# Strassen's scheme for four more blocks of the down projection in the first feed-forward group

## The chip, the cores and the metric

The kernel runs on one core of one Trainium2 chip, in one launch. The time is the device time of that launch in microseconds (us). Beside it stands a profile of one execution on the same chip. The engines: PE multiplies matrices and loads its weights by instructions of their own (PEld), DVE and ACT do elementwise work, POOL some small copies, and SP issues most of the DMA transfers. Every engine takes its own instructions in order and waits at semaphores for the others.

## The reference

One step of a hybrid encoder layer over 2048 prompt tokens and 64 sample tokens, with a model width of 1024. The change touches only the second half, the gated feed-forward with a causal convolution of width 3 (`d_ff` = 2816):

```python
h2 = rmsnorm(x, g2) * (1 + sc2) + sh2
up = h2 @ w_up                                  # 1024 -> 2 * 2816
conv = b_conv + sum(w_conv[j] * upp[:, j:j + T] for j in range(3))
a, g = jnp.split(conv, 2, -1)
x = x + gt2 * ((jax.nn.silu(g) * a) @ w_down)   # 2816 -> 1024
```

All of it is float32. The kernel splits each operand into a high and a low part and takes three matmuls for each product of two blocks (high by high, high by low, low by high).

## The kernel before

The first third of the span is the attention and pooling half. Then the 2112 tokens run through the feed-forward in three groups (`fgroups`, `o.g` = 0, 1, 2) of 704 tokens. Channels lie on the partitions, tokens on the free axis. The 2816 hidden channels are 22 blocks of 128 (`f` = 0 to 21), and each block has an up-projection pair, one half for `a` and one for `g`.

**Up.** `Pair.products` (L1701) computes one pair by seven products in place of eight (Strassen's scheme in Winograd's form; the weight sums are ready in HBM as `wsum`, the sums of the activations in `B`). A product is 12 matmuls of 128x352, at L1604, and takes one "unit" of weights: 512 columns, loaded by SP, copied to the high part by ACT (L427), and turned into the low part by DVE (L430, "split" below). In group 0 all seven units of a pair are split, and three of them stored for the later groups (`wsplit`); groups 1 and 2 load those three as they are and split four. The results are taken from PSUM by DVE (`sum_g1` and `sum_a`, L1613, writing `eg` and `ea`) and ACT, run through the convolution (DVE L1582, four of them for a pair), Silu (ACT L1801), the gate (DVE L1806 or L1809), and a split into high and low (ACT L1884 and DVE L1889) into a tile called `av`. The steps of a pair lie in the products of the next one and the one after.

**The order of a pair's evacuation.** At the start of a pair its first product B11 is issued on PE; then come `sum_g1` and `sum_a` of the pair before. PE needs the first of them two products later, since the last product (T4) of the pair before goes into the same PSUM bank, and the second for a free bank.

**Down.** `PARTS` (L33) cuts the 22 blocks into parts. For group 0 they are (0, 5), (5, 10), (10, 16), (16, 22). After the pairs of a part its blocks are multiplied by `w_down`. A plain part is `down` (L2199): for each of 8 output blocks, each hidden block, two token ranges (448 and 256) and three passes, one matmul at L2212. A part of exactly four blocks (`NQ`) in groups 1 and 2 is a quad: its four blocks and the 8 output blocks are two Strassen products (`quad_down`, L2046), 14 half products of 6 matmuls of 128x352 for each, at L2073. It is held until after the first pair of the next part, whose evacuation is woven into it. A quad needs more of DVE and ACT: sums of the blocks and their splits (`step_2` to `step_7`, L1817, L1821, L1833) before it, and 24 additions to the residual in place of 16 behind it (`rows_add`, L2042).

**The sums of the quads' weights.** The four sums of each quad's weights are computed in the kernel by `quad_sums` (L1654): 10 pieces `d` (two for a quad), each in two column halves, 20 units in all. A unit is a load of 512 KB from `w_quad` into a tile of the `av` pool, four DVE operations of 128x256 on it (tile name `qs`, L1664 to L1670), and a store of 512 KB to `dsum`. It is a generator in the background list `bg[0]`: each `tick(0)` runs it to the next `yield`. A product ticks it twice (`if kc % 2: tick(0)`), a plain `down` once in every 12 matmuls. In `bg[1]` runs `prepare`, which makes the next group's activations and their sums (DVE L747, L784, L780 on `fscr`). `drain(i)` runs a list to its end.

**What sets the order.** PE, ACT, DVE and POOL keep the order of the program (`manual_schedule`, L2032); only SP's order is chosen by a scheduler. Weights are loaded up to seven units ahead and split up to three ahead (`ahead[:] = [7, 4, WB, 1]`); `wt` tiles number 7, `raw` tiles 5, `av` tiles 7, PSUM banks for this work 6.

Of the kernel before, what the change touches and what calls it, by code (L numbers as in the profile page):

```python
# [31 lines left out]
ENDS = ((0, 448), (448, 704))  # L32
PARTS = (((0, 5), (5, 10), (10, 16), (16, 22)), ((0, 4), (4, 8), (8, 12), (12, 16), (16, 20), (20, 22)),  # L33
         ((0, 4), (4, 8), (8, 12), (12, 16), (16, 22)))
NQ, QUADS = 4, 5


def paired(g, part):
    return g > 0 and part[1] - part[0] == NQ
EPS = 1e-6  # L40
# [25 lines left out]
def tile_layer(ctx: ExitStack, tc: tile.TileContext, xT, vecs, cst, rst, w_mod, w_ada, w_qkou, w_v, w_pool,  # L66
# [38 lines left out]
    bg = ([], [], [], [], [])  # L105
# [1547 lines left out]

    def quad_sums():  # L1654

        for d in range(2 * QUADS):
            for c in (0, 256):
                t = f2.tile([P, 2, FT], F32R, tag="av", name="qs", bufs=AVB)
                w = t.bitcast(F32).rearrange("p a t -> p (a t)")[:, :1024].rearrange("p (i c) -> p i c", i=4)
                nc.sync.dma_start(out=w, in_=w_quad[d, :, :, c:c + 256])  # L1660
                for _ in range(5):
                    yield
# [10 lines left out]
                nc.sync.dma_start(out=dsum[d, :, :, c:c + 256], in_=w)  # L1673
                yield
                yield
# [476 lines left out]
    for o in fgroups:  # L2152
        Bo = B[o.g]
        held = None
        for pi, part in enumerate(PARTS[o.g]):
# [4 lines left out]
            av = [None] * nf  # L2160
            quad = Quad() if paired(o.g, part) else None
            if pi == 0:
                pair = None
            for f in range(f0, f1_):
                old, pair = pair, Pair(o, Bo, f, f - f0, av, quad)
                pair.products(old)
                if o.g == 0 and len(x3) < KD or pi == 0 and not bg[0]:
                    x3 += load_x2(o, range(len(x3), min(len(x3) + 2, KD)))
                if held is not None and nf > 2:
                    quad_down(o, held, pair, old)  # L2170
                    held = None
            if pi == 0 and o.g > 0:
                drain(0)
                x3 += load_x2(o, range(len(x3), KD))
            if not o.last:
                if pi == 0:
                    if o.g == 0:
                        bg[0].append(quad_sums())
                    bg[1].append(prepare(fgroups[o.g + 1], fscr))
                if lastp:  # L2180
                    drain(0, 1)
                    if nf == 2:
# [94 lines left out]
        if not o.last:  # L2277
            drain(1)
            if nf == 2:
                Bn = B[-1]  # L2280
                Bn.load(BN[-1])
            bg[0].append(final(o, x3, ssum, nf == 2))
            x3 = []
# [87 lines left out]
```

## Time and profile before

| what | value |
| --- | --- |
| median of 3 runs | 2170.43 us (2169.34 to 2173.03) |
| the profiled execution's own time | 2169.81 us |
| its span, first to last instruction | 2168.0 us |
| group 0's pairs and down parts | from 789 to 1252 us of the span |
| PE busy in 745 to 1257 us | 510.66 of 512.00 us |
| DVE busy in 745 to 1257 us | 396.88 of 512.00 us |
| ACT busy in 745 to 1257 us | 281.42 of 512.00 us |
| share of the DMA engines' time in 745 to 1257 us | 0.83, at 285 GB/s |
| granted PE clock there | 1.00 |

A row of the windows view names a stretch of the span, its length, then each engine's busy time with the number of its instructions, the granted PE clock, the share of the DMA engines' time and the rate. A row of the timeline has a start, a duration, the engine, the line, the operation, the tiles and shapes, and in brackets the idle time just before it with what ended it. Two operations of one engine can overlap in their records: the distance from one start to the next is what the engine needed. A row of the chain of waits has a start, a length, and the engine and line that set the end there.

### The profile page before, as it was taken

What the parts mean: (1) busy time and instruction counts of PE and PEld (TensorE: products, weight loads), DVE (VectorE), ACT (ScalarE), POOL (GpSimd) and SP (SyncE); (2) the same over time, 40 slices, a digit from 0 to 9 for tenths busy, and PEclk for the clock granted to TensorE, in tenths of its full rate; (3) what the DMA queues carried; (4) which work ended last, traced back from release to release, by engine and by line L of the source; (5) the groups of instructions that cost most, each with busy time, mean ns of one, the idle gap of its engine ahead of it and who ended that gap; (6) DMA issues with size and microseconds to landing.
All of it is one profiled execution on the core that took longest, in us unless ns stands there. A gap on an engine that the chain in (4) does not pass through costs nothing.

```text
span 2168.0 us, 38128 instructions
## 1 busy us (share of the span) xinstructions
PE 2146.5 (99%) x13529; PEld 2040.9 (94%) x13529; DVE 1666.4 (77%) x3107; ACT 1104.1 (51%) x2201; POOL 249.3 (12%) x468
## 2 busy tenths in 40 slices
PE   8999999999999999999999999999999999999998
PEld 7888888888899999999999999999999999999998
DVE  5777678677675878797968668988888797887874
ACT  4554335334333556464736445655656455565554
POOL 0010000001000301010101220100101121111112
PEclk9999999999999999999999999999999999999999
DMA  8987997897788686888968976666666875555542
GB/s 317 330 307 228 321 317 252 282 320 269 246 286 281 229 268 232 293 288 301 353 235 307 319 264 206 226 227 200 219 232 230 277 269 190 171 175 188 173 157 76
DMA packets 302439, 545.28 MB, mean 252 GB/s; under 512 B 25984, under 2 KB 118656, under 8 KB 302248
## 3 DMA queue, kind: packets, MB, share of 16 engines
q1 hardware_dynamic: 291656, 517.64, 70.6%
q10 hardware_dynamic: 10592, 25.20, 3.0%
q8 instruction: 107, 1.75, 0.3%
q14 instruction: 84, 0.69, 0.1%
HBM read 414.65 MB, written 128.08 MB: 250 GB/s over the span
## 4 chain that ended last, share of the span: by engine, by line
PE 60%; DVE 3%; DMA 1%; issue 1%; ACT 1%; POOL 0%; SPq 0%; DVEq 0%; POOLq 0%; ACTq 0%
PE mm L1604 37%; PE mm L2212 11%; PE mm L2073 10%; PE mm L494 2%; DVE wt L430 1%; DVE tg L1582 0%; ACT tg L1577 0%; DMA wt<-dsum 0%; DMA wt<-wsum 0%; DMA fscr<-h2d 0%; DVE ea L1613 0%; DVE eg L1613 0%; DVE x L2042 0%; DVE tg L1809 0%; ACT mm L1652 0%
## 5 line engine op out<-in xcount | busy, mean ns | idle before, releaser
L1604 PE MATMUL mm<-hx,wt 128*128 128x352 f32 x5544 | 887.1, 321 | 0.9 <-DVE wt L430 0.7
L1604 PEld LDWEIGHTS mm<-hx,wt 128*128 128x128 f32 x5544 | 880.5, 188 | 2.2 <-DVE wt L430 1.9
L494 PE MATMUL mm<-hl,wt 128*128 128x512 f32 (+2 forms) x1920 | 385.8, 356 | 0.3 <-DMA wt<-hl_kept 0.3
L427 ACT ACTIVATE wt<-raw 128x512 fp32r<-128x512 f32 (+3 forms) x468 | 275.9, 597 | 191.0 <-PE mm L494 53.4
L430 DVE TENSOR_TENSOR wt<-raw,wt 128x512 fp32r<-128x512 f32 (+3 forms) x468 | 307.3, 663 | 74.8 <-ACT wt L427 73.3
L494 PEld LDWEIGHTS mm<-hl,wt 128*128 128x128 f32 x1920 | 314.7, 188 | 48.1 <-issue 4.4
L2073 PE MATMUL mm<-av,wt 128*128 128x352 f32 x1512 | 248.2, 324 | 2.7 <-DVE ea L1613 1.2
L2073 PEld LDWEIGHTS mm<-av,wt 128*128 128x128 f32 x1512 | 242.3, 188 | 6.2 <-DVE ea L1613 4.0
L2042 DVE SCALAR_TENSOR_TENSOR x<-mm,MOD,x 128x352 f32<-128x352 f32 (+5 forms) x384 | 180.3, 508 | 69.0 <-PE mm L2212 54.1
L2212 PE MATMUL mm<-av,wt 128*128 128x448 f32 (+1 forms) x1440 | 232.2, 322 | 0.0
L2212 PEld LDWEIGHTS mm<-av,wt 128*128 128x128 f32 x1440 | 221.2, 188 | 9.9
L1652 ACT ACTIVATE mm<-mm 128x352 f32<-128x352 f32 x204 | 91.4, 448 | 235.9 <-PE mm L1604 176.6
L494 PE MATMUL mm<-mx,wt 128*128 128x512 f32 (+1 forms) x960 | 182.2, 351 | 1.2 <-DVE scr L266 1.2
L494 PEld LDWEIGHTS mm<-mx,wt 128*128 128x128 f32 x960 | 158.5, 188 | 24.1 <-DVE scr L266 1.1
L1582 DVE SCALAR_TENSOR_TENSOR ta<-ea,V,ta 128x704 f32<-128x704 f32 (+1 forms) x132 | 125.6, 952 | 54.8 <-ACT ta L1577 48.2
L1582 DVE SCALAR_TENSOR_TENSOR tg<-eg,V,tg 128x704 f32<-128x704 f32 (+1 forms) x132 | 125.7, 952 | 50.5 <-ACT tg L1577 48.0
L430 DVE TENSOR_TENSOR wt<-wt 128x512 fp32r<-128x512 f32 x204 | 138.4, 683 | 11.6 <-ACT wt L427 11.6
L427 ACT ACTIVATE wt<-wt 128x512 fp32r<-128x512 f32 x204 | 123.6, 622 | 34.0 <-DMA wt<-wsum 31.0
L1560 POOL COPY ea<-UC 128x2 f32<-128x2 f32 x66 | 32.7, 496 | 510.4 <-DVE ta L1582 429.1
L1801 ACT ACTIVATE tg<-tg 128x704 f32<-128x704 f32 (+1 forms) x66 | 52.4, 794 | 69.3 <-DVE tg L1582 69.3
L1143 PE MATMUL mm<-wt,hl 128*128 128x256 f32 (+1 forms) x576 | 71.2, 284 | 0.0
L1143 PEld LDWEIGHTS mm<-wt,hl 128*128 128x128 f32 x576 | 70.2, 189 | 0.8 <-issue 0.6
(306 smaller groups left out, 2220.2 us busy)
## 6 DMA issues: line engine op xcount, KB each, us to landing
wt<-wsplit SPq DMA_DIRECT2D x132, 512.0 KB, 4.3
raw<-w_up SPq DMA_DIRECT2D x198, 256.0 KB, 4.3
wt<-hl_kept SPq DMA_DIRECT2D x96, 512.0 KB, 6.3
wt<-wsum SPq DMA_DIRECT2D x132, 256.0 KB, 5.2
wsplit<-wt SPq DMA_DIRECT2D x66, 512.0 KB, 5.4
w<-w_up SPq DMA_DIRECT2D x88, 256.0 KB, 4.8
wsum<-w SPq DMA_DIRECT2D x44, 512.0 KB, 6.0
Bd<-fscr ACTq DMA_DIRECT2D x56, 352.0 KB, 4.4
```

The source lines that it names most:

```text
L427: act.activation(u.w[:, 0, :u.n], u.raw[:, :u.n], AF.Copy)
L430: dve.tensor_tensor(out=u.w[:, 1, :u.n], in0=u.raw[:, :u.n], in1=u.w[:, 0, :u.n].bitcast(F32), op=ALU.subtract)
L494: pe.matmul(ps[bi][:, :hi - lo], U[:, a, k % 4 * P:(k % 4 + 1) * P], mv[k][:, b, lo:hi], start=(at == 0 and pi == 0), stop=(k == order[-1] ...
L1143: pe.matmul(ps[ti][:n, :cols], h[4 * kh + k4][:, b, lo:lo + n], U[:, a, k4 % 2 * cols:(k4 % 2 + 1) * cols], start=(kh == 0 and k4 == 0 and ...
L1560: pool.tensor_copy(ext[:, 0:2], UC[:, f, :])
L1582: dve.scalar_tensor_tensor(out=t[:, :E], in0=ext[:, j:j + E], scalar=wc(j, f), in1=t[:, :E], op0=ALU.mult, op1=ALU.add)
L1604: pe.matmul(bk.t[:, :FH], U[:, a, kc * P:(kc + 1) * P], Bo.at(nm, kc, b), start=(first and kc == 0 and pi == 0), stop=(kc == 3 and pi == 2 ...
L1652: act.activation(to.t[:, :FH], bk.t[:, :FH], AF.Copy)
L1801: act.activation(self.tg[:, :E], self.tg[:, :E], AF.Silu)
L2042: dve.scalar_tensor_tensor(out=x3[n][:, a:b], in0=bk.t[:, a - lo:b - lo], scalar=gt2(n, s), in1=x3[n][:, a:b], op0=ALU.mult, op1=ALU.add)
L2073: pe.matmul(bk.t[:, :FH], U[:, a, c:c + P], quad.put(op, m, b), start=(first and m == 0 and pi == 0), stop=(m == 1 and pi == 2), skip_grou ...
L2212: pe.matmul(bks[i].t[:, :hi - lo], U[:, a, k % 4 * P:(k % 4 + 1) * P], av[k][:, b, lo:hi], start=(k == 0 and (a, b) == PASSES[0]), stop=(k ...
```

## The change

Group 0's parts become (0, 6), (6, 12), (12, 16), (16, 22), and the quad scheme is allowed for group 0 too, so that blocks 12 to 15 are a quad. Its weight sums (`d` = 6 and 7) must exist before, so the list of `quad_sums` is cut in two: `SUMS[0]` = pieces 6, 7, 0, 1, 2, 3 from the end of part 0's pairs on, and `SUMS[1]` = pieces 4, 5, 8, 9 after the quad has been multiplied. A `drain(0)` stands ahead of the quad's first pair, another after group 0's end. A unit of the list has 11 steps where it had 13 (4 empty ones for 5 after the load, 2 for 3 after the store).

```diff
-PARTS = (((0, 5), (5, 10), (10, 16), (16, 22)), ((0, 4), (4, 8), (8, 12), (12, 16), (16, 20), (20, 22)),
+PARTS = (((0, 6), (6, 12), (12, 16), (16, 22)), ((0, 4), (4, 8), (8, 12), (12, 16), (16, 20), (20, 22)),
          ((0, 4), (4, 8), (8, 12), (12, 16), (16, 22)))
 NQ, QUADS = 4, 5
+SUMS = ((6, 7, 0, 1, 2, 3), (4, 5, 8, 9))
 def paired(g, part):
-    return g > 0 and part[1] - part[0] == NQ
+    return part[1] - part[0] == NQ
...
-    def quad_sums():
-
-        for d in range(2 * QUADS):
+    def quad_sums(ds):
+
+        for d in ds:
             for c in (0, 256):
...
                 nc.sync.dma_start(out=w, in_=w_quad[d, :, :, c:c + 256])
-                for _ in range(5):
+                for _ in range(4):
                     yield
...
                 nc.sync.dma_start(out=dsum[d, :, :, c:c + 256], in_=w)
-                yield
                 yield
                 yield
...
             quad = Quad() if paired(o.g, part) else None
+            if quad is not None and o.g == 0:
+                drain(0)
...
                     quad_down(o, held, pair, old)
                     held = None
+                    if o.g == 0:
+                        bg[0].append(quad_sums(SUMS[1]))
...
                     if o.g == 0:
-                        bg[0].append(quad_sums())
+                        bg[0].append(quad_sums(SUMS[0]))
                     bg[1].append(prepare(fgroups[o.g + 1], fscr))
                 if lastp:
-                    drain(0, 1)
+                    drain(1) if o.g == 0 else drain(0, 1)
...
             drain(1)
+            if o.g == 0:
+                drain(0)
```

The program has 12 970 matmuls where it had 12 994: 168 more of 128x352 at the quad's line, 96 fewer of 128x448 and 96 fewer of 128x256. DVE has 3129 instructions for 3109, ACT 2217 for 2205 (eight PSUM copies more among them), SP 1540 for 1542. Lines behind the first edit are numbered one higher than before.

The first place is DVE in part 1, from one pair's evacuation (`eg`, `ea`) on. Before, in pair 6's work:

```order
L1613 TENSOR_TENSOR eg<-mm,s_10058 128x352
L1613 TENSOR_TENSOR ea<-mm,s_10058 128x352
L1806 TENSOR_TENSOR tg<-ta,tg 128x704
L430 TENSOR_TENSOR wt<-wt 128x512
L1889 TENSOR_TENSOR av<-tg,av 128x704
L430 TENSOR_TENSOR wt<-raw,wt 128x512
L1664 TENSOR_TENSOR qs<-qs 128x256
L1582 SCALAR_TENSOR_TENSOR ta<-ea,V,ta 128x704 x2
L430 TENSOR_TENSOR wt<-wt 128x512
L1666 TENSOR_TENSOR qs<-qs 128x256
```

The change, in pair 7's work (the second of its part, as pair 6 was before):

```order
L1614 TENSOR_TENSOR eg<-mm,s_10259 128x352
L1614 TENSOR_TENSOR ea<-mm,s_10259 128x352
L1806 TENSOR_TENSOR tg<-ta,tg 128x704
L431 TENSOR_TENSOR wt<-wt 128x512
L1665 TENSOR_TENSOR qs<-qs 128x256
L1667 TENSOR_TENSOR qs<-qs 128x256
L1889 TENSOR_TENSOR av<-tg,av 128x704
L431 TENSOR_TENSOR wt<-raw,wt 128x512
L1669 TENSOR_TENSOR qs<-qs 128x256
L1671 TENSOR_TENSOR qs<-qs 128x256
L1583 SCALAR_TENSOR_TENSOR ta<-ea,V,ta 128x704 x2
```

From this `eg` to the next one DVE has 24 instructions (7 of them `qs`), where it had 21 (4 `qs`); the next three distances have 23, 24 and 22 where the longest ones of the old part 1 had 21 and 23, and those of the old part 2 (pairs 10 to 15) 21, 21, 23 and 22.

The second place is DVE at the start of the new quad: what stands between `eg` of pair 15 and `eg` of pair 16, which is now inside `quad_down`. Of its 25 instructions these are the last:

```order
L1583 SCALAR_TENSOR_TENSOR tg<-eg,V,tg 128x704 x2
L785 TENSOR_TENSOR fscr<-fscr 128x352
L781 TENSOR_TENSOR fscr<-fscr 128x352
L431 TENSOR_TENSOR wt<-raw,wt 128x512
L431 TENSOR_TENSOR wt<-wt 128x512
L785 TENSOR_TENSOR fscr<-fscr 128x352
L781 TENSOR_TENSOR fscr<-fscr 128x352 x2
L1809 TENSOR_TENSOR tg<-ta,tg 128x704
L1821 TENSOR_TENSOR tg<-tg 128x352 x2
L431 TENSOR_TENSOR wt<-raw,wt 128x512
L1614 TENSOR_TENSOR eg<-mm,s_12117 128x352
L1614 TENSOR_TENSOR ea<-mm,s_12117 128x352
```

Before, pairs 15 and 16 lay on the two sides of a plain down part, and the end of pair 15's distance was:

```order
L784 TENSOR_TENSOR fscr<-fscr 128x352
L430 TENSOR_TENSOR wt<-raw,wt 128x512 x2
L1664 TENSOR_TENSOR qs<-qs 128x256
L1666 TENSOR_TENSOR qs<-qs 128x256
L784 TENSOR_TENSOR fscr<-fscr 128x352
L780 TENSOR_TENSOR fscr<-fscr 128x352
L430 TENSOR_TENSOR wt<-raw,wt 128x512
L430 TENSOR_TENSOR wt<-raw,wt 128x256
L1613 TENSOR_TENSOR eg<-mm,s_11866 128x352
```

What moved: no `qs` stands between pairs 12 and 16 any more, and in their place stand the gate, the differences of blocks (L1821) and their splits.

## The prediction

> **What bounds the kernel now.** I read the page's totals first, then the chain of waits through group 0, then the windows there pair by pair, and last the timeline of DVE.
>
> ```profile
> PE 2146.5 (99%) x13529; PEld 2040.9 (94%) x13529; DVE 1666.4 (77%) x3107; ACT 1104.1 (51%) x2201; POOL 249.3 (12%) x468
> ```
>
> PE is busy all the time but 21.5 us of the 2168.0, so time can only be won by taking matmuls away, and every new wait of PE costs its full length. What a matmul costs in a row of many is in the chain, whose pieces have a start, a length, a line and a count:
>
> ```profile
> 894.79 36.11 PE mm L1604 x228
> ...
> 1000.34 77.92 PE mm L1604 x492
> ...
> 1084.15 41.98 PE mm L2212 x264
> ...
> 1325.18 23.05 PE mm L2073 x144
> ```
>
> So an up matmul takes 77.92 / 492 = 0.158 us, a plain down matmul (448 and 256 columns by turns) 41.98 / 264 = 0.1590, one of a quad 23.05 / 144 = 0.1601. A pair of 7 x 12 matmuls is 84 x 0.158 = 13.3 us of PE.
>
> The whole-span 77% of DVE hides that DVE is full where the change puts work. The windows of one pair's length, first in the old part 1, then in the old part 2 (stretch, length, busy PE, PEld, DVE, ACT, POOL, clock, DMA share, GB/s):
>
> ```profile
> 934.00:947.00 13.00, 13.00 (x84) 12.98 (x83) 12.57 (x21) 10.02 (x19) 2.41 (x4) 1.00 0.95 323
> 947.00:960.00 13.00, 12.88 (x81) 12.57 (x80) 12.86 (x23) 9.75 (x18) 2.13 (x4) 1.00 0.96 349
> ...
> 1065.00:1078.00 13.00, 13.00 (x84) 13.00 (x83) 12.53 (x22) 9.37 (x18) 2.13 (x4) 1.00 1.01 351
> ```
>
> DVE works 12.5 to 12.9 of 13 us late in a part; PE loses its first 0.12 us at 947 to 960. I measure how late DVE is by the start of `eg`, which can start when the next pair begins on PE:
>
> ```profile
> 906.29 0.53 DVE L1613 TENSOR_TENSOR eg<-mm,s 128x352 f32<-128x352 f32 x1 [0.69 <-PE mm L1604]
> 920.44 0.52 DVE L1613 TENSOR_TENSOR eg<-mm,s 128x352 f32<-128x352 f32 x1
> 934.89 0.52 DVE L1613 TENSOR_TENSOR eg<-mm,s 128x352 f32<-128x352 f32 x1
> 948.21 0.52 DVE L1613 TENSOR_TENSOR eg<-mm,s 128x352 f32<-128x352 f32 x1
> ...
> 1067.46 0.52 DVE L1613 TENSOR_TENSOR eg<-mm,s 128x352 f32<-128x352 f32 x1
> ```
>
> The part's first pair has six products (72 matmuls, 11.4 us), so pairs begin at 894.8 + 11.4 = 906.2 and then 919.5, 932.8 and 946.1. DVE is late by 0.1, 0.9, 2.1 and 2.1 us. What followed is in the waits of 895 to 960 us, one weight load that a split held up for 0.4 us:
>
> ```profile
> PEld mm L1604 <- DVE wt L430: 0.4, 1, 0.4
> ```
>
> In the old part 2 `eg` of pair 14 started at 1067.46, when pair 15 had begun at 1000.34 + (72 + 4 x 84) x 0.158 = 1064.95: 2.5 us late, and the last window above shows no loss. I take 2.5 us as what PE tolerates (2.1 to 3.3: the upper end is where T4 comes, two products or 3.8 us after the pair's start, less the 0.5 us of `eg`).
>
> **The change part by part.**
>
> *PE.* 192 plain matmuls go, 168 come: 192 x 0.1590 = 30.53 us less, 168 x 0.1601 = 26.90 us more, in sum -3.6 us. No other matmul is added, and the banks that `take(True)` hands out are already written widely enough. This is the whole gain there can be: 0.17%.
>
> *DVE's price of each operation*, from one start to the next:
>
> ```profile
> 1053.29 0.52 DVE L1613 TENSOR_TENSOR eg<-mm,s 128x352 f32<-128x352 f32 x1
> 1053.73 0.51 DVE L1613 TENSOR_TENSOR ea<-mm,s 128x352 f32<-128x352 f32 x1
> 1054.16 0.88 DVE L1806 TENSOR_TENSOR tg<-ta,tg 128x704 f32<-128x704 f32 x1
> 1054.96 0.69 DVE L430 TENSOR_TENSOR wt<-wt 128x512 fp32r<-128x512 f32 x1
> 1055.56 0.42 DVE L1668 TENSOR_TENSOR qs<-qs 128x256 f32<-128x256 f32 x1
> 1056.01 0.42 DVE L1670 TENSOR_TENSOR qs<-qs 128x256 f32<-128x256 f32 x1
> 1056.36 0.88 DVE L1889 TENSOR_TENSOR av<-tg,av 128x704 fp32r<-128x704 f32 x1
> 1057.16 0.68 DVE L430 TENSOR_TENSOR wt<-raw,wt 128x512 fp32r<-128x512 f32 x1
> 1057.76 1.93 DVE L1582 SCALAR_TENSOR_TENSOR ta<-ea,V,ta 128x704 f32<-128x704 f32 x2
> 1059.61 0.95 DVE L747 SCALAR_TENSOR_TENSOR fscr<-fscr,G,rb 128x704 f32<-128x704 f32 x1
> 1060.47 1.29 DVE L430 TENSOR_TENSOR wt<-wt 128x512 fp32r<-128x512 f32 x2
> ...
> 1065.06 0.52 DVE L784 TENSOR_TENSOR fscr<-fscr 128x352 fp32r<-128x352 f32 x1
> 1065.62 0.52 DVE L780 TENSOR_TENSOR fscr<-fscr 128x352 f32<-128x352 f32 x1
> ```
>
> Evacuation 0.44, gate and low part 0.80, split 0.60, `qs` 0.40, two taps 1.85, L747 0.86, L784 and L780 about 0.5. A steady pair without background needs 2 x 0.44 + 2 x 0.80 + 7 x 0.60 + 2 x 1.85 = 10.4 us.
>
> *Denser sums in part 1.* By the counts of the change, DVE needs between one `eg` and the next, from pair 7 on: 10.4 + 7 x 0.40 + 2 x 0.86 = 14.9; 10.4 + 5 x 0.40 + 3 x 0.5 = 13.9; 10.4 + 4 x 0.40 + 5 x 0.5 = 14.5; with an eighth split 11.0 + 4 x 0.40 + 2 x 0.5 = 13.6. Against 13.3 each that is 3.7 us too much in four pairs. (The old part 1 by the same prices: 13.7 and 13.0 in the two distances that took 14.45 and 13.32; idle time behind ACT is the rest.) From a lag of 0.9 us, as every part had after its second pair, and with 0.2 to 0.4 us more in all for ACT, the lag would be 0.9 + 3.7 + 0.3 = 4.9 us; less the tolerated 2.5, PE waits 2.4 us. Bounds: 0.8 with a tolerance of 3.3 and the last distance falling into the down part, where DVE catches up; 4.0 if each distance keeps the 0.5 us of idle time behind ACT that the old ones had on average.
>
> *The quad's steps.* Pairs 12 to 15 have no `qs`, but blocks to subtract and split. No quad stands in group 0 before; its operations have the shapes of rows above (352 columns 0.44, 704 columns 0.80). From pair 14's `eg`: 14.4 us to pair 15's, 15.1 us to pair 16's, which lies in the quad. With a lag of 0.9 at pair 14's, it is 2.0 at 15's, and pair 16's `eg` starts 2.0 + 15.1 - 13.3 = 3.8 us after the quad's start Q; `ea` ends 0.95 later. What that costs is shown by the third quad of group 1, which starts at 1479.87:
>
> ```profile
> 1479.87 3.05 PE L2073 MATMUL mm<-av,wt 128*128 128x352 f32 x18
> 1483.68 1.23 PE L2073 MATMUL mm<-av,wt 128*128 128x352 f32 x6 [0.77 <-DVE ea L1613]
> ...
> 1482.68 0.52 DVE L1613 TENSOR_TENSOR eg<-mm,s 128x352 f32<-128x352 f32 x1
> ```
>
> There `eg` came at Q + 2.8 and the fourth half product waited 0.77 us for a bank. At Q + 3.8 it waits 1.8. Bounds: 0.4 (`eg` at Q + 2.4, no lag at all) and 3.0 (0.5 us of idle time in each of the two distances). Inside the quad DVE has 62 instructions up to the next pair's evacuation for 40.2 us of PE; 38.5 us even by recorded durations, so it catches up.
>
> *Costed at nothing.* The `drain(0)` ahead of pair 12 finds one unit of the list unfinished: its four `qs` stand in a row, 1.6 us, while DVE has its slack of a part's first pair (0.1 us late at 906.29, where a down part lay just before); without that cover 1.6 us. Second half of the list: 6 `qs` or fewer on 10.4 us, so at most 12.8 us a pair, under PE's 13.3. The loads on SP that stand behind a store of the list wait for it, which was so before too:
>
> ```profile
> SPq L1660 <- DMA dsum<-qs: 7.3, 3, 2.8
> ```
>
> Three such waits then (7.3 us in all), four now; SP runs seven units, 13 us, ahead of PE. ACT gains 8 copies and 4 other instructions in some 60 us and has 3 of 13 us free.
>
> *Sum.* -3.6 + 2.4 + 1.8, and the 0.12 us wait of the old part 1 goes: +0.5 us on a span of 2168.0, which stands for 2169.81 of time; the median, 2170.43, lies 0.6 above that execution. So 2170.9 us.
>
> A rule of the Trainium skill speaks against even this. VectorE: DVE Perf Modes, section "The DRAIN you can't avoid", says that the next DVE instruction starts only when the pipeline of the one before is empty, though it lets one "that is not held" start earlier. The rows above have starts 0.44 us apart for records of 0.52, so the trace takes the exception's side.
>
> **Rivals.**
>
> *DVE keeps up (2166.7).* PE saves its 3.6 us and waits no more than now: 2170.43 - 3.7. For it: in the old part 2 a lag of 2.5 us cost nothing, and the tolerance could be 3.3 or more; the down parts give DVE time back. Against it: 12.86 of 13 us busy already, and 3.7 us more asked for than four pairs hold.
>
> *ACT and the transfers stretch DVE's chain (2176.9): the slower side.* In part 1 the DMA share is 0.95 and 0.96 in the windows from 934 to 960, in the old part 2 it reaches 1.01. A unit of the list moves 1 MB; at 14 ticks a pair the list went at 14/13 units a pair and goes now at 14/11, 0.2 MB more, 0.57 us of transfers at 350 GB/s. Weights then land later, ACT waits for them, and DVE waits for ACT before it can split:
>
> ```profile
> ACT wt L427 <- DMA wt<-wsum: 7.8, 5, 2.0
> ```
>
> That is ACT's wait in the old part 2's 1000 to 1079 us. If each saturated pair (five in part 1, three around the quad) loses the 0.75 us by which the first one of the old part 1 exceeded its work (14.45 against 13.7), 6.0 us come on top: 2176.9, and with two thirds of it the end is still over 4.3 us slower. It decides from about 0.5 us a pair. Against it: saturated distances (13.32 for 13.0) had little idle time left, and the quad's own pairs move less, with no list running.
>
> *No overlap on DVE (2178).* If operations cost their recorded durations, some 0.075 us more each, the four pairs need 93 x 0.075 = 7.0 us more, the two distances of the quad 48 x 0.075 = 3.6 us; cut by what idle time they replace I count 7 us. The rows of starts exclude it for the steady pairs. This is what the page's rule would make without its exception.
>
> That the saving itself fails is no rival: the matmul counts are fixed by the program.
>
> **How the numbers follow.** The forecast, gain and waits about equal, 0.47 (2168 to 2173.5); DVE keeps up, 0.24; ACT and transfers, 0.26; no overlap, 0.03. I call no change what lies within 0.2%, 4.3 us, about what a measurement of this kernel can tell. Slower by more: most of the last two, 0.24, and the forecast's upper tail, 0.03: 0.27. Faster by more than the 3.6 us that PE can save takes a favourable scatter on top of the first rival: 0.10. The same: 0.63. The range holds from the first rival's 2166.7 less a little scatter nearly to the second's: 2166.3 to 2176.5.
>
> **What would show it.** Right: PE's matmul time down by 3.6 us; windows of part 1's pairs with DVE at 12.8 or more of 13 us and PE losing about 2 us there, its waits ended by DVE's L1613 or L430; `eg` more than 2.5 us late from pair 8 or 9 on; in the new quad a wait of 1 to 3 us before its fourth half product. Wrong: PE windows of 13.00 throughout group 0 (then the tolerance was more than I took, and the time is near 2167), or waits of PE that transfers end, or waits outside of group 0.

## The result, and the profile after

| | median | lowest to highest |
| --- | --- | --- |
| after | 2181.94 us, 6 runs | 2179.85 to 2183.42 |
| before, beside it | 2170.76 us, 6 runs | |
| ratio | 1.0050 | 95% interval 1.0037 to 1.0063 |

The change costs 11 us. The forecast was 2170.9 with a range to 2176.5, so the truth lies outside of it, on the slower side.

The page's totals of the kernel after (engine, busy us, share of the span, instructions), from an execution with a span of 2178.9 us:

```profile
PE 2147.9 (99%) x13505; PEld 2040.8 (94%) x13505; DVE 1679.6 (77%) x3127; ACT 1112.6 (51%) x2213; POOL 250.3 (11%) x468
```

PE has 24 matmuls less and yet 1.4 us more of busy time, so waits are not all: some matmuls got longer. The timeline of PE's matmuls in group 0 says where (start, length, count, and in brackets the wait just before with what ended it):

```profile
917.83 66.54 PE L1605 MATMUL mm<-hx,wt 128*128 128x352 f32 x410
986.12 14.83 PE L1605 MATMUL mm<-hx,wt 128*128 128x352 f32 x82 [1.75 <-DVE wt L431]
1000.78 4.03 PE L2216 MATMUL mm<-av,wt 128*128 128x448 f32 x24
...
1048.53 52.01 PE L1605 MATMUL mm<-hx,wt 128*128 128x352 f32 x326
1102.22 13.26 PE L1605 MATMUL mm<-hx,wt 128*128 128x352 f32 x82 [1.68 <-DVE wt L431]
1115.31 3.40 PE L2073 MATMUL mm<-av,wt 128*128 128x352 f32 x18
1121.06 1.24 PE L2073 MATMUL mm<-av,wt 128*128 128x352 f32 x6 [2.35 <-DVE ea L1614]
...
1147.08 12.10 PE L1605 MATMUL mm<-hx,wt 128*128 128x352 f32 x74
1159.75 40.17 PE L1605 MATMUL mm<-hx,wt 128*128 128x352 f32 x252 [0.57 <-DVE wt L431]
1201.05 9.78 PE L1605 MATMUL mm<-hx,wt 128*128 128x352 f32 x60 [1.12 <-DVE wt L431]
1212.50 3.75 PE L1605 MATMUL mm<-hx,wt 128*128 128x352 f32 x22 [1.68 <-DVE wt L431]
1216.09 4.31 PE L2216 MATMUL mm<-av,wt 128*128 128x448 f32 x24
```

Each stretch against its matmuls at the prediction's prices (0.1584 us for an up matmul, 0.1601 for one of a quad):

| stretch | took | its matmuls | excess | predicted |
| --- | --- | --- | --- | --- |
| pairs of part 1, 917.83 to 1000.78 | 82.95 | 492 up: 77.9 | 5.0 | 2.4 (0.8 to 4.0) |
| pairs 12 to 16 and the quad, 1048.53 to 1147.08 | 98.55 | 420 up, 168 quad: 93.4 | 5.1 | 1.8 (0.4 to 3.0) |
| pairs 17 to 21, 1147.08 to 1216.09 | 69.01 | 408 up: 64.6 | 4.4 | 0 |

That is 14.5 us; less the 3.6 us of saved matmuls, 10.9, which is the result (11.2) but for scatter. The first stretch holds the pairs 6 to 11, the second the pairs 12 to 16 and the quad. The saving is real, and three stretches give it back four times over.

Two views show what is behind these waits. The windows of part 1's pairs (stretch, length, PE, PEld, DVE, ACT, POOL busy, then granted clock, DMA share, GB/s):

```profile
917.00:957.00 40.00, 40.00 (x257) 40.00 (x256) 30.26 (x51) 25.22 (x45) 4.72 (x8) 1.00 1.00 349
957.00:970.00 13.00, 12.88 (x80) 12.31 (x78) 12.52 (x22) 10.14 (x19) 2.13 (x4) 1.00 1.02 377
970.00:986.00 16.00, 14.35 (x84) 13.72 (x84) 14.50 (x26) 9.96 (x19) 2.13 (x4) 1.00 1.03 369
986.00:1001.00 15.00, 14.88 (x84) 14.87 (x85) 14.60 (x27) 9.97 (x19) 2.25 (x4) 0.89 0.97 332
```

The DMA engines are full through all of part 1's pairs, and DVE is busy three quarters of the first 40 us and then nearly all the time. The last row also has the longer matmuls: 84 of them in 14.88 us, where 13.3 is normal, at a mean granted clock of 0.89.

And the timeline of DVE at the end of pairs 17 to 21:

```profile
1206.33 0.68 DVE L431 TENSOR_TENSOR wt<-raw,wt 128x512 fp32r<-128x512 f32 x1
1209.57 0.43 DVE L1665 TENSOR_TENSOR qs<-qs 128x256 f32<-128x256 f32 x1 [2.56 <-DMA qs<-w_quad]
1209.91 1.93 DVE L1583 SCALAR_TENSOR_TENSOR ta<-ea,V,ta 128x704 f32<-128x704 f32 x2
1211.76 0.68 DVE L431 TENSOR_TENSOR wt<-wt 128x512 fp32r<-128x512 f32 x1
```

For 2.56 us DVE waits, by the trace for a load of the list, and behind it in DVE's order stand two taps and the split that PE is waiting for: PE starts again at 1212.50. The chain of waits has the same place (start, length):

```profile
1194.51 7.41 DMA wt<-wsum
...
1203.06 6.49 DMA qs<-w_quad
```

This load took 6.49 us from its issue to its landing, and its first sum stands four empty steps behind the issue, some 4 us by 14 steps in a pair of 13.3. The loads land no later than they did: the median of the list's 20 loads is 6.1 us in the kernel after and 6.7 in the kernel before. In 917 to 1222 us of the kernel after, DVE's waits for such loads are the second largest:

```profile
DVE x L2042 <- PE mm L2216: 13.0, 11, 1.8
DVE qs L1665 <- DMA qs<-w_quad: 9.5, 6, 2.6
```

(us in all, times, longest; the first row is in the down parts, where DVE has little to do.) Of the 9.5 us, 2.0 fall into part 1's pairs, 2.3 into the quad's stretch, 4.9 into the pairs 17 to 21 and the rest into the down parts. The kernel before has no such row.

### The profile page after: what moved, and what is told of

The parts are those of the page before. It is cut to its first block, busy times and chain, and to the rows that moved or that the text cites. A ratio compares the mean times of both kernels' runs of the same rounds, so it can differ in the third digit from the quotient of the medians.

```text
span 2178.9 us, 38101 instructions
## 1 busy us (share of the span) xinstructions
PE 2147.9 (99%) x13505; PEld 2040.8 (94%) x13505; DVE 1679.6 (77%) x3127; ACT 1112.6 (51%) x2213; POOL 250.3 (11%) x468
## 4 chain that ended last, share of the span: by engine, by line
PE 54%; DVE 5%; DMA 3%; issue 2%; ACT 2%; POOL 0%; SPq 0%; DVEq 0%; ACTq 0%; POOLq 0%
PE mm L1605 32%; PE mm L2073 11%; PE mm L2216 9%; PE mm L495 2%; DVE wt L431 2%; DVE tg L1583 1%; DMA wsplit<-wt 1%; ACT tg L1578 1%; DMA wt<-dsum 0%; DMA wt<-wsum 0%; DVE ta L1583 0%; DVE eg L1614 0%; DVE ea L1614 0%; DMA qs<-w_quad 0%; DMA fscr<-h2d 0%
## 5 line engine op out<-in xcount | busy, mean ns | idle before, releaser
L428 ACT ACTIVATE wt<-raw 128x512 fp32r<-128x512 f32 (+2 forms) x458 | 273.6, 604 | 178.6 <-PE mm L495 51.3
L431 DVE TENSOR_TENSOR wt<-raw,wt 128x512 fp32r<-128x512 f32 (+2 forms) x458 | 305.2, 673 | 70.7 <-ACT wt L428 70.3
L2073 PE MATMUL mm<-av,wt 128*128 128x352 f32 x1680 | 275.9, 324 | 4.6 <-DVE ea L1614 2.8
L2042 DVE SCALAR_TENSOR_TENSOR x<-mm,MOD,x 128x352 f32<-128x352 f32 (+4 forms) x392 | 184.2, 509 | 59.5 <-PE mm L2216 43.4
L2216 PE MATMUL mm<-av,wt 128*128 128x448 f32 (+1 forms) x1248 | 201.3, 322 | 0.0
L431 DVE TENSOR_TENSOR wt<-wt 128x512 fp32r<-128x512 f32 x212 | 143.6, 683 | 10.8 <-ACT wt L428 10.8
L428 ACT ACTIVATE wt<-wt 128x512 fp32r<-128x512 f32 x212 | 128.7, 622 | 26.3 <-DMA wt<-wsum 22.6
L1578 ACT ACTIVATE tg<-eg,V 128x704 f32<-128x704 f32 (+1 forms) x66 | 64.5, 977 | 13.6 <-DVE tg L1821 11.3
```

Source lines behind the costliest of these rows:

```text
L428: act.activation(u.w[:, 0, :u.n], u.raw[:, :u.n], AF.Copy)
L431: dve.tensor_tensor(out=u.w[:, 1, :u.n], in0=u.raw[:, :u.n], in1=u.w[:, 0, :u.n].bitcast(F32), op=ALU.subtract)
L1578: act.activation(t[:, :E], ext[:, 2:2 + E], AF.Identity, scale=wc(2, f), bias=V[:, V_BC + f:V_BC + f + 1])
L2042: dve.scalar_tensor_tensor(out=x3[n][:, a:b], in0=bk.t[:, a - lo:b - lo], scalar=gt2(n, s), in1=x3[n][:, a:b], op0=ALU.mult, op1=ALU.add)
L2073: pe.matmul(bk.t[:, :FH], U[:, a, c:c + P], quad.put(op, m, b), start=(first and m == 0 and pi == 0), stop=(m == 1 and pi == 2), skip_grou ...
L2216: pe.matmul(bks[i].t[:, :hi - lo], U[:, a, k % 4 * P:(k % 4 + 1) * P], av[k][:, b, lo:hi], start=(k == 0 and (a, b) == PASSES[0]), stop=(k ...
```

## The experiments

Each kernel is timed against the kernel before on the same chip, whose median was between 2171.0 and 2173.3. Costs in us are the ratio less one, times 2171. A stretch that is some us "over its matmuls" is priced as in the table above.

### One part of the change alone, or one less

**More time for the list's loads.** The changed kernel with five empty steps after the load, as before.

```diff
-                for _ in range(4):
+                for _ in range(5):
                     yield
```

> The change with five empty steps instead of four between a unit's load and its first DVE operation (12 steps a unit, not 11); nothing else. Theory L (DVE, in order and nearly full, stands still for loads of the list that have not landed; the profile of the change shows 13.0 us of such waits in 7 places, that of before none): most of these waits go and with them 5 to 8 us of the 11, so 2174 to 2177 us. Theory W (DVE simply has more work than time around pairs 7 to 16, as my forecast said, only under-priced): the operations stay, only the densest pair loses 3 of 7, so 1 to 2 us at most come back, 2180 to 2181. Theory D (the bunch that the drain makes ahead of pair 12): the bunch grows (15 operations after pair 11's evacuation for 12), so it stays or gets worse, 2181 to 2184.

Measured: 2185.05, ratio 1.0062 (1.0047 to 1.0077): slower, but not where the step was meant to help. In the pairs 17 to 21 DVE's waits for the list's loads fell from 4.9 us to 1.1, and PE ran through without a wait, 65.2 us for 408 matmuls (0.6 over), at a DMA share of 0.90 where the changed kernel has 0.87:

```profile
1158.12 65.36 PE L1605 MATMUL mm<-hx,wt 128*128 128x352 f32 x408
```

The list gets longer, though, and what is left of it at the `drain(0)` ahead of pair 12 stands in a bunch on DVE. There DVE stood 4.95 us at a load of the list, and PE lost the most:

```profile
1060.86 48.68 PE L1605 MATMUL mm<-hx,wt 128*128 128x352 f32 x288 [3.77 <-DVE wt L431]
```

So the drain is no free place, though in the changed kernel itself it costs next to nothing (0.4 us in the 326 matmuls from 1048.53 on).

**Without the list's sums.** The four `dve.tensor_tensor` of a unit become empty steps (the weight sums are left out); loads and stores stay.

> The change with the list's four DVE operations left out of every unit: the blocks are loaded and stored as they come, at the same steps, so the quads multiply blocks where they should multiply sums. No DVE operation is there to work or to wait, all transfers stay. Theories L and W both expect the time of PE's saving less what the quad's own steps cost: 2167 to 2170 us. If transfers are what is late (theory T), it stays above 2175. If the quad's own steps are most of it (theory Q), 2172 to 2176, with PE waiting in pairs 14 to 16 and at the quad's start still.

Measured: 2176.65, ratio 1.0027 (1.0018 to 1.0037), half of the loss gone. Pairs 17 to 21 took their 64.98 us for 408 matmuls, without a wait. Part 1's pairs were 2.4 us over their matmuls. The wait for a load did not vanish with the sums: SP now stood 33.6 us at the list's stores until the loads had landed (910 to 1230 us). The quad kept both of its waits, and its stretch was 7.0 over:

```profile
1100.59 13.26 PE L1605 MATMUL mm<-hx,wt 128*128 128x352 f32 x82 [1.67 <-DVE wt L431]
...
1119.72 1.90 PE L2066 MATMUL mm<-av,wt 128*128 128x352 f32 x6 [2.34 <-DVE ea L1614]
```

**The shorter steps alone**, on the kernel before (4 for 5 empty steps after the load, 2 for 3 after the store).

> The kernel before, with the change's step counts alone (4 empty steps after a unit's load, 2 after its store; one list, no quad in group 0). Theory L: DVE waits for loads here too, about 0.6 us for each of 20 units, and in pairs 5 to 15, which are full, part of it reaches PE: 2173 to 2177 us. Theory W: the same work a little earlier, one pair with 7 operations of the list: 2170 to 2172. Theory D says nothing of it.

Measured: 2177.71, ratio 1.0032 (1.0021 to 1.0044). The denser list alone costs 7 us.

**The new cut alone**, on the kernel before (parts of 6, 6, 4 and 6 blocks, all plain).

```diff
-PARTS = (((0, 5), (5, 10), (10, 16), (16, 22)),
+PARTS = (((0, 6), (6, 12), (12, 16), (16, 22)),
```

> The kernel before with the new parts of group 0 alone (0-6, 6-12, 12-16, 16-22; the part of four blocks multiplied plainly, the list as before with 13 steps). Every theory but one expects no change, 2170 to 2172 us: the matmuls are the same and DVE has the same work. If the longer first two parts are to blame by themselves (more pairs in a row at full DVE), 2173 or more, with PE waiting in pairs 9 to 11.

Measured: 2181.51, ratio 1.0046 (1.0031 to 1.0061): as slow as the whole change, with no quad at all. I had not expected that. The costs don't add: 7 us and 10 us alone, 11 us with the quad on top. By PE's timeline part 1's pairs were 4.9 us over their matmuls, with 1.16 us more just behind them, and the pairs 12 to 15 with their plain down part 5.7 (89.49 us from 1048.28 on). Most of the latter are two waits in that down part, for the evacuation and the `av` tile of the part's last pair:

```profile
1104.03 2.14 PE L1604 MATMUL mm<-hx,wt 128*128 128x352 f32 x12 [1.78 <-DVE eg L1613]
...
1114.76 0.47 PE L2212 MATMUL mm<-av,wt 128*128 128x448 f32 x1 [1.87 <-ACT av L1884]
```

The pairs 16 to 21 behind it were clean, 77.9 us for 492 matmuls. So the part of four blocks loses some 5 us in group 0 even when it is multiplied plainly.

### How much DVE has to do

**The sums left out elsewhere.** The kernel before without the list's sums, and the new cut without them.

> The kernel before, with the four VectorE sums of every unit of the list left out (about 26 us of VectorE in group 0); loads, stores and parts stay. It leaves out the weight sums, so later groups read unsummed weights. Theory C (VectorE's work between two evacuations sets how late it is, and TensorE pays what exceeds about 2.5 us): before loses only 0.1 us in group 0, so 2168.5 to 2171. Theory A (any new order of this program costs some microseconds, whatever it does to VectorE): 2175 or more, as the kernel with only longer steps did.

> The kernel before with the new cut of group 0 into parts (6, 6, 4, 6 blocks, no Strassen there) and with the four VectorE sums of every unit of the list left out. It leaves out the weight sums. With them this cut took 2181.5. Theory C (VectorE's work): the waits of part 1 and of the four-block part go, 2169 to 2172. Theory S (the cut itself, a four-block part with its short down part and six blocks behind it): the loss in the four-block part stays, 5 us or more, and only part 1 is mended: 2175 to 2178.

Measured: 2171.40 for the first, ratio 0.9992 (0.9982 to 1.0002): the kernel before has nothing to gain from them. The second 2175.78, ratio 1.0014 (1.0004 to 1.0023): with the sums the cut costs 10 us, without them 3. In the second one's trace part 1's pairs are still 2.6 us over their matmuls, and the pairs 12 to 15 with their down part 3.4.

**More sums.** The kernel before with six operations a unit for four.

```diff
                 dve.tensor_tensor(out=a12, in0=a12, in1=a11, op=ALU.subtract)
+                dve.tensor_tensor(out=a12, in0=a12, in1=a11, op=ALU.add)
+                dve.tensor_tensor(out=a12, in0=a12, in1=a11, op=ALU.subtract)
```

> The kernel before, with two more operations of 128x256 in each of the list's twenty units (an addition and its subtraction again, 0.80 us a unit, 16 us in all; the weight sums differ by rounding alone). Theory C: before's pairs in parts 1 and 2 have no room, so each of some seven full pairs loses up to 0.8 us less what the tolerance of 2.5 us takes: 2174 to 2178. Theory X: VectorE's added work is hidden, 2170 to 2172.

Measured: 2177.54, ratio 1.0024 (1.0013 to 1.0034). So 16 us of added DVE work cost 5: work alone counts too, where DVE is full.

**Less of other work.** The changed kernel with the low part of every second stored unit cut short.

```diff
-            dve.tensor_tensor(out=u.w[:, 1, :u.n], ...)
+            n = 64 if spare and u.keep is not None and u.at % 2 == 0 else u.n
+            dve.tensor_tensor(out=u.w[:, 1, :n], ...)
```

> The changed kernel, with VectorE's half of the split of every second weight unit of group 0 made on 64 of its 512 columns (about 70 of 142 operations, 0.45 us each, 31 us of VectorE spread evenly; the low parts of these weights are left out). Parts, list, quad, transfers and ACT's work stay. Theory C: PE's waits in group 0 go almost wholly and the 3.6 us of saved matmuls come out, 2167 to 2170. Theory X (the loss lies in the order, ACT's copies, buffers and transfers, and VectorE is late only because it waits for them): at least half of the 14 us of waits stay, 2174 or more.

Measured: 2182.51, ratio 1.0048 (1.0036 to 1.0061): nothing came back. It hit fewer units than I had counted: only stored ones, and 111 of 142 splits in 917 to 1222 us stayed long. Still some 14 us of DVE went (31 by about 0.45), and PE's waits stayed at their places, the quad's at their lengths (1.67 and 2.34 us). The pairs 17 to 21 were 3.7 us over, where it had been 4.4. Of what DVE won, some 6 us went into longer waits for the list's loads and behind ACT's copies, which were 9.5 and 8.8 us in the changed kernel:

```profile
DVE wt L432 <- ACT wt L428: 13.4, 15, 2.1
...
DVE qs L1666 <- DMA qs<-w_quad: 11.2, 5, 3.2
```

That is where the theory of mere work fell as the whole account: taking the list's sums away helps, taking away 14 us of other work does not.

### Other queues and other orders

**The sums on GpSimd, and the list's transfers on GpSimd's queue**, each in the changed kernel.

> The changed kernel, with the list's four sums on GpSimd in place of VectorE (about 26 us of VectorE's work moved to an engine that is 12% busy). Theory C: as the changed kernel without these sums, 2175 to 2178, the rest being the cost of the Strassen product's own steps. Theory P (GpSimd's operations slow VectorE's at the same time): 2180 or more, with VectorE's splits longer than 0.68 us while GpSimd works.

> The changed kernel, with the list's loads and stores issued from GpSimd's queue in place of SP's. Theory H (SP's stores of the list wait for VectorE's sums and hold the weight loads that stand behind them, which makes ACT and VectorE later still): 2171 to 2176, and SP's waits for VectorE's qs (17.9 us in group 0) are gone with the waits for weights. Theory C (VectorE's work alone): 2180 to 2184, SP's waits gone without PE gaining anything.

Measured: 2195.51, ratio 1.0108 (1.0090 to 1.0125), and 2247.61, ratio 1.0353 (1.0332 to 1.0373). Neither tests what it was meant to. GpSimd's order also holds the small copies of the convolution, which DVE's taps need. In the first kernel GpSimd stood 71.3 us at the list's loads, SP 36.9 us at the stores behind GpSimd's sums (17.9 behind DVE's in the changed kernel), and ACT 46.9 us for weights (13.3), all in 917 to 1222 us; which of these cost the 23 us is not shown. In the second kernel GpSimd stood at the stores, and DVE at the loads, by the waits of the same stretch:

```profile
POOL dsum L1674 <- DVE qs L1671: 91.6, 12, 18.4
...
DVE qs L1665 <- DMA qs<-w_quad: 49.0, 10, 9.9
```

**The stores later.** The two empty steps behind the list's store moved ahead of it.

> The changed kernel, with the two empty steps that stood behind each store of the list put ahead of it: as many steps, but the store is issued two steps (2 to 3 us) later, when VectorE's last sum of the unit is done. Theory H (SP stands at the store until VectorE is done, and the weight loads behind it come late, which makes VectorE later still): SP's waits for VectorE's sums in group 0 fall from 17.9 us to under 6, and the time to 2176 to 2179. Theory C (VectorE's work between two evacuations alone): SP's waits fall too, the time stays at 2181 to 2184.

Measured: 2185.54, ratio 1.0066 (1.0053 to 1.0078). SP's waits for the last sum, in the changed kernel and then here, where the store stands on line 1676:

```profile
SPq L1674 <- DVE qs L1671: 17.9, 9, 4.6
...
SPq L1676 <- DVE qs L1671: 14.3, 9, 2.3
```

They got shorter and did not go, and the time did not fall. So the run does not show that SP's standing at these stores costs nothing; how much of the loss it makes stays open.

**The order at the quads.** The current pair's two sums ahead of the done pair's gate, in the changed kernel and in the kernel before.

```diff
+        cur.sum_g1()
+        cur.sum_a()
         done.gate()
         done.step_2()
...
-            if d == 0:
-                cur.sum_g1()
-                cur.sum_a()
```

> The changed kernel with the current pair's two sums (eg, ea) issued ahead of the done pair's gate and first subtractions at every quad's start. Theory O: in the quad of group 0 PE waits 2.3 us for ea, which stands in VectorE's order behind the gate, two subtractions and splits, about 3 us of work; ahead of them it comes 2 us or more earlier, and the wait goes: 2178.5 to 2180, and the quads of the later groups, which lose 4.0 us in nine weight loads behind ea in the kernel before, gain up to 4 us more: down to 2175. Theory C: the gate and the operands T2 and B21 come later instead and PE waits for them: 2181 to 2184.

> The kernel before with the two sums ahead of the gate at the start of each of its nine quads. Theory O: 1 to 4 us faster, 2167 to 2170, from nine weight loads that wait 4.0 us in all for ea. Theory C: no change (2170 to 2172), since these quads' VectorE has time to spare and what is won is lost by the later gate.

Measured: 2185.87, ratio 1.0064 (1.0050 to 1.0078), and 2175.28, ratio 1.0018 (1.0009 to 1.0027): slower in both. The 2.35 us wait is gone, and PE waits in its place for what now comes later; in the first kernel, whole span:

```profile
PE mm L2075 <- DVE wt L431: 5.5, 8, 1.2
```

**A fourth buffer for the scaled halves**, first with smaller operand tiles to make room, alone and together with the last edit, then with the room from elsewhere.

```diff
-        t = f1.tile([P, EX], F32, tag="t", name="t" + tag, bufs=3)
+        t = f1.tile([P, EX], F32, tag="t", name="t" + tag, bufs=4)
```

> The changed kernel with a fourth buffer for the tiles that the gate's two halves are scaled into (ta and tg, three before); the tiles of the block operands shrink a little to make room. Theory T: in the quad's pairs both gated tiles are kept until T4 is split, so ACT's scaling waits for a buffer that VectorE's subtraction frees (1.99 us at 1095.9 in the run without sums), the taps come late and PE waits 1.68 us once before the quad's first product, in every kernel with a quad in group 0. With a fourth buffer this wait goes: 2178.5 to 2180.5. Theory C (VectorE has too much work there in any case): the wait stays within 0.5 us or moves behind the quad's start: 2181 to 2183.

> Both of the last two edits. If both theories hold: 2174 to 2178, and what is left over the 2167.5 that the matmuls alone would give is the part ahead of the quad (5 us) and the pairs behind it (4.4 us), where the list's sums run. If VectorE's work sets the loss whatever the order: 2180 or more.

> The changed kernel with a fourth buffer for the scaled halves ta and tg, and the block operands' tiles as they were: the room comes from the tile of the final convolution state, whose two halves now go to the carried state's tile (so that output's two halves are both its last). In the earlier run with a fourth buffer the smaller operand tiles made every up matmul slower, which hid the effect. Theory T: the 1.68 us wait ahead of the quad shrinks to about 0.4 and the rest stays: 1 to 2 us under the changed kernel, 2180 to 2181, 8 to 9 us over before. Theory N (what the quad's order makes late is only shifted): the quad stretch stays at 98.5 us and the time at 2182 to 2184.

Measured: 2190.02, ratio 1.0087 (1.0073 to 1.0100); 2194.43, ratio 1.0101 (1.0087 to 1.0115); 2181.77, ratio 1.0043 (1.0029 to 1.0057). In the first two all up matmuls are longer (last section). In the third DVE's idle time behind ACT ahead of the quad is mended (1.18 us in the changed kernel, none there), and so is the 1.68 us wait, but in the profile the pairs 12 to 16 end no sooner: 67.69 us from their start to the quad's, where it was 66.78.

```profile
1052.03 67.85 PE L1604 MATMUL mm<-hx,wt 128*128 128x352 f32 x408
1119.72 3.29 PE L2072 MATMUL mm<-av,wt 128*128 128x352 f32 x18
```

PE shows no wait in this row; its matmuls took 0.166 us each in place of 0.158 at a granted clock of 1.00, and what held them the profile does not show. (The profiled execution took 2184.63 us, 2.9 over its kernel's median.) So the missing buffer makes the 1.68 us wait, and giving it one did not make the kernel faster beyond the scatter.

### The list's bytes, and their place

**A quarter of the load.** The changed kernel with only the first of four blocks of a unit loaded (the weight sums are left out), the four DVE operations made of it, stores whole.

```diff
-                nc.sync.dma_start(out=w, in_=w_quad[d, :, :, c:c + 256])
+                nc.sync.dma_start(out=w[:, 0], in_=w_quad[d, :, 0, c:c + 256])
```

> The changed kernel, with the list loading only the first of the four blocks of each unit and making its four VectorE operations of it: a quarter of the load's bytes, 0.63 of the list's traffic, with VectorE's, SP's and ACT's work and order as they were (the weight sums are left out). Theory B (the transfers are full in the pairs of part 1, DMA share 1.00 at 354 GB/s from 917 to 1000 us, so loads land late and VectorE, whose order is fixed, stands behind them: 13 us for the list's loads alone): VectorE's waits for the list fall under 5 us, PE's waits in part 1 and in pairs 17 to 21 fall by half or more, 2174 to 2178; the quad's own 5 us stay. Theory O (the order alone, with no part for the transfers): 2180 to 2184.

Measured: 2177.05, ratio 1.0024 (1.0015 to 1.0033), as good as without the sums, though DVE does every operation of the changed kernel. DVE's waits for the list shrank from 9.5 us to

```profile
DVE qs L1665 <- DMA qs<-w_quad: 0.3, 2, 0.2
```

and PE's waits in group 0 to these, besides three under 0.6 us:

```profile
984.35 9.77 PE L1605 MATMUL mm<-hx,wt 128*128 128x352 f32 x60 [1.10 <-DVE wt L431]
...
1099.92 13.93 PE L1605 MATMUL mm<-hx,wt 128*128 128x352 f32 x82 [1.68 <-DVE wt L431]
...
1119.64 1.23 PE L2073 MATMUL mm<-av,wt 128*128 128x352 f32 x6 [2.33 <-DVE ea L1614]
```

Part 1's pairs took 81.15 us (3.2 over their matmuls), the quad's stretch 99.4 (6.0 over), pairs 17 to 21 65.7 (1.1 over). Fewer bytes make the list's loads land in time, and the whole DMA share of part 1's pairs falls from 1.00 to 0.94; which of the two counts more this run can't tell. For the pairs 17 to 21 the first run above can: there the loads kept their bytes and got one step more, and the loss went too.

**The list in the down parts.** No step of the list in pairs 6 to 15, half of them in pairs 17 to 21, and one step more at each tick of group 0's down parts.

```diff
-            if kc % 2:
+            if kc % 2 and kc >= pace[0]:
                 tick(0)
...
                         tick(1 - c // len(secs) % 2)
+                    if o.g == 0:
+                        tick(0)
```

> The changed kernel, with the list moved out of the pairs: no step of it in the pairs 6 to 15, a step at every second tick of the pairs 17 to 21, and one more step at each tick of group 0's down parts, where the DMA share is 0.64 to 0.70 and VectorE has a quarter of its time free. The sums per down part go from 12 to 24 operations. Theory B: part 1 and the pairs 17 to 21 are clean, the 9 us that they lose come back, and the quad's own 5 us stay: 2171 to 2175. Theory O: part 1 keeps 2 us or more of waits, 2176 or more. If the down parts have no room after all, PE waits there for weights: 2180 or more.

Measured: 2205.08, ratio 1.0153 (1.0139 to 1.0167). The pairs 17 to 21 are clean (64.98 us for their 408 matmuls). The others are not: part 1's took 83.4 us (5.5 over their matmuls), with 1.1 us of waits of PE among them, and the pairs 12 to 16 took 69.9 (5.2 over). The down parts lost more still, with waits of 4.5 and 5.4 us at the end of the first two. There a step now comes every 4 matmuls, where it came every 12 (and every 6 in a pair), so four empty steps are some 2.5 us, and DVE stood at the list (780 to 1285 us):

```profile
DVE qs L1666 <- DMA qs<-w_quad: 47.7, 9, 7.5
```

The DMA share was only 0.65 and 0.64 in most of the first two down parts (868 to 917 and 1000 to 1048 us). So full transfers are not needed for the wait: the distance from a load to its first use, in DVE's fixed order, is enough.

None of these kernels beats the kernel before.

## Why the prediction was wrong

**PE saves 3.6 us: right.** The matmul counts and prices hold; where nothing waits, as in pairs 17 to 21 without the list's sums, 408 up matmuls took 64.98 us, within 0.4 us of the price.

**Denser sums in part 1: right in place, half in size.** 2.4 forecast, 5.0 measured, over the upper bound of 4.0. The waits came late in the part and a split ended them, as said. The undisturbed pairs would begin at 942.5, 955.8, 969.1 and 982.4, and DVE's `eg` came 0.4, 3.0, 4.0 and 6.4 us later:

```profile
942.95 0.52 DVE L1614 TENSOR_TENSOR eg<-mm,s 128x352 f32<-128x352 f32 x1
...
958.84 0.52 DVE L1614 TENSOR_TENSOR eg<-mm,s 128x352 f32<-128x352 f32 x1
...
973.11 0.52 DVE L1614 TENSOR_TENSOR eg<-mm,s 128x352 f32<-128x352 f32 x1
...
988.83 0.51 DVE L1614 TENSOR_TENSOR eg<-mm,s 128x352 f32<-128x352 f32 x1
```

The distances are 15.9, 14.3 and 15.7 us, where I had 14.9, 13.9 and 14.5: 2.6 us more. The work in them was counted nearly right, and the idle time was not: DVE waited 2.5 us in them, 1.8 of it behind ACT and 0.7 at a load of the list, and I had allowed 0.3 for all. Another 1.6 us of the 5.0 are matmuls at a granted clock of 0.89, which I had no term for. That the denser list is what made part 1 lose is not shown, though: the new cut with the old list lost as much there (4.9).

**The quad's steps: mis-sized, 1.8 for 5.1.** I foresaw the wait at the fourth half product (2.35 us, bounds 0.4 to 3.0) and not the 1.68 us ahead of the quad. These rows of DVE's timeline are the kernel after:

```profile
1096.94 0.52 DVE L1821 TENSOR_TENSOR tg<-tg 128x352 f32<-128x352 f32 x1
1098.63 1.94 DVE L1583 SCALAR_TENSOR_TENSOR tg<-eg,V,tg 128x704 f32<-128x704 f32 x2 [1.18 <-ACT tg L1578]
...
1104.16 0.51 DVE L1614 TENSOR_TENSOR eg<-mm,s 128x352 f32<-128x352 f32 x1
1104.59 0.51 DVE L1614 TENSOR_TENSOR ea<-mm,s 128x352 f32<-128x352 f32 x1
...
1120.06 0.52 DVE L1614 TENSOR_TENSOR eg<-mm,s 128x352 f32<-128x352 f32 x1
```

From pair 15's `eg` to pair 16's it is 15.9 us where I had 15.1, and `eg` came at Q + 4.75 where I had Q + 3.8. I had summed DVE's operations with no idle time between them. In the quad DVE and ACT work in turn on three buffers: ACT's scaling waits 1.98 us for the subtraction at L1821, and DVE's taps 1.18 for ACT. The 2.3 us wait was in every kernel that kept the quad and its order, with the list's sums, without them, with lighter splits and with lighter loads. The stretch of the quad was 5.1, 6.0 and 7.0 us over its matmuls (as it is, with light loads, without sums).

That does not make these microseconds the quad's own. The same part of four blocks, multiplied plainly, was 5.7 us over with the sums and 3.4 without. The whole of group 0, by PE's timeline, lasted 450.3 us before, 461.5 with the cut alone and 460.7 with the change; without the sums 455.6 with the cut and 455.7 with the change. By the times, quad and shorter steps cost 0.9 us on top of the cut with the sums and 2.8 without, and the intervals overlap in both cases. So what they lose on top of the cut is about what the saved matmuls bring, and a loss nearly as large as the change's comes with the cut alone.

**The step that failed: what I "costed at nothing".** "6 `qs` or fewer on 10.4 us, so at most 12.8 us a pair, under PE's 13.3" counts the operations and not the load ahead of them. Pairs 17 to 21 lost 4.4 us, with 1.68 us of it at the end of the chain shown above, 1203.06 to 1212.50. Four runs hold this: without the sums these pairs were clean; with a quarter of the load, and every operation kept, nearly so (1.1 us); with one step more ahead of the first sum, and every byte and operation kept, too (0.6 us); and with lighter splits they still lost 3.7 us. The cut alone, with the old steps and the old list, lost nothing in these pairs. The zero for the drain held only because the list was nearly done there.

The new cut was put at nothing as well, without being named: the prediction has no term for parts of 6, 6, 4 and 6 blocks as such, and alone they cost 10 us.

**The rivals.** "ACT and transfers stretch DVE's chain", 2176.9 with a chance of 0.26, came nearest and was still 5 us too low. Late transfers were part of it, but not by the path that I gave: ACT's waits for `wsum` loads were 13.3 us in 917 to 1222 us, and 16.5 in the kernel before. What DVE waited for were the list's own loads. "DVE keeps up" is out. "No overlap on DVE" is out by the same rows as before: in pair 15's distance `eg` to `ea` is 1104.16 to 1104.59, for records of 0.51 us, so the exception in the Trainium skill's page VectorE: DVE Perf Modes, section "The DRAIN you can't avoid", still describes this trace better than its rule.

**What stays open.** Why the new cut loses 10 us. Its trace says where (part 1, and the down part behind pair 15), but DVE's waits for the list were only 2.6 us there, and no run took the loads alone away from it. Without the sums 3 us are left of the 10. Nor is it settled what SP's standing at the list's stores costs, nor how part 1's loss divides between the cut and the denser list.

## What to carry to other kernels

Before an engine that keeps its program's order takes background work, ask for each operation not only how long it lasts but whether its operand will be there. A load needs its worst landing time between issue and first use, counted in time and not in steps, since steps shrink where the code around them does.

Where an engine and the DMA engines are both at 0.95 or more of a stretch, take no edit there as free: re-cutting the parts alone, shortening the list's steps alone and two more operations a unit alone each cost 5 to 10 us here. A gain of 0.17% should not be bought with steps in such a stretch.

## What the hardware showed that I had not expected

After waits of 1.7 to 2.4 us, PE sometimes ran the following matmuls slower: 84 in 14.88 us with a mean granted clock of 0.89, where 13.3 us is normal. There, behind the 1.75 us wait, the clock was 0.50 from 987.5 to 989 us and 1.00 again from 991 us on. It didn't always: after the 2.35 us wait at 1121.06 six matmuls took 1.24 us, and 1.90 us after the same wait in the kernel without sums.

The step from one row of the block operands to the next in SBUF seems to matter to PE. With the smaller operand tiles (376 floats for 384, and the data's offset 24 for 32) the same 414 up matmuls took 66.68 us where they take 65.82 in the changed kernel, 1.3% longer, while the down matmuls, which read other tiles, show the usual length, 30.10 us for 189, as in the changed kernel. The fourth buffer is not the reason, since with it and the old tiles the 414 took 65.82 us again; what else moved in SBUF with the smaller tiles was not tested.

```profile
804.10 66.68 PE L1605 MATMUL mm<-hx,wt 128*128 128x352 f32 x414
...
889.55 30.10 PE L2216 MATMUL mm<-av,wt 128*128 128x256 f32 x189
```

GpSimd took 0.95 to 1.07 us (means by line) for a sum of 128x256 that takes DVE 0.42.
